# A hybrid decoder step: branch A's products behind the C tiles, gate A's as filler, the sample states' update in four row tiles

## The chip, the cores and the metric

The kernel runs on one core of one Trainium2 chip. The metric is the device time of one execution in microseconds. A profiled execution gives a span, from the first instruction to the last, and a time of its own, which is a little longer. TensorE (PE) multiplies, VectorE (DVE) and ScalarE (ACT) do the elementwise work, GpSimd (POOL) and SyncE (SP) issue most of the transfers.

## The reference

One layer of a decoder for 288 positions (256 of a new prompt, and 8 samples of 4 new tokens each), in float32. One projection of the normalised input gives the channels of both branches and their gates; all weights are read once, so the work is large products with 288 columns. Cut to what matters here:

```python
h = rmsnorm(x, norm1_g)
s_in, z, xbc, dt_raw, ga, gb = split(h @ w_in)
ya = sgu_branch(s_in, ...)                     # branch A: u * (W_s LN(v) + b)
yb, h_new, ... = mamba_branch(z, xbc, dt_raw, conv_buf, h0, ...)   # branch B: conv, SSD scan, gate, norm
merged = sigmoid(ga) * (ya @ w_out_a) + sigmoid(gb) * (yb @ w_out_b)
x = x + merged @ w_o
# SwiGLU feed-forward, final norm
```

For each of the 8 samples, 64 heads and a state of 64 x 128 per head, the recurrent state is also brought up to date over the sample's 4 tokens: the old state times the decay over the four tokens, plus the sum over the tokens of (decayed x dt) times B. This is some 16 MB read and as much written:

```python
h_fin = dec[..., None, None] * h + states     # states = einsum over the tokens of b, decay, x * dt
```

## The kernel before

**Float32 products.** Each operand is split into a high half (a float32r cast) and a low half (the rest), and a product is three matmuls: high x high, low x high, high x low. Weights are split as they arrive: SP loads a block `raw` (128 x 4 x 256), ACT casts it to `wh`, DVE subtracts to `wl`. A tile of 256 output channels takes 16 blocks of 128 input channels, two halves and three matmuls: 96 matmuls of 288 columns into the PSUM tile `pm`. The input is in such halves too: `hh`/`hl` for h, `yah`/`yal` for branch A, `ybh`/`ybl` for branch B, `mgh`/`mgl` for the merged branches, `xgh`/`xgl` and `fh`/`fl` for the feed-forward.

**Order.** `_order` lists the tiles: v (branch A), dt and b, u, c (C of the scan), ga (gate A), A (branch A's projection), then x and z tiles of the eight head groups of branch B between b tiles, B (first half of branch B's projection, which needs groups 0 to 3), further x and z tiles, gb, and B's second half. The output projection and the feed-forward follow. `units` runs through this list and issues the matmuls of the tiles, one after the other. After every block of a tile it calls `side`, which gives each waiting generator (an evacuation, a head group's scan, a state update) one step. The class `Plan` keeps a clock for each engine, adds a cost for each instruction that it issues, and holds a generator back until what it needs is ready by these clocks: so the order of each engine's instructions is fixed when the program is built. In it a load is ready 4000 ns after the transfer clock (`load`, lines 196 to 199), whichever queue issues it, and issuing takes the queue no time. Matmuls then wait for what really arrives.

**Branch A and its gate.** `g_gate_a` leaves tanh of half the gate in `sga`; `g_a` multiplies the product of a tile with it on DVE (line 170 is the helper's) and stores it to `scr_a`. `g_b2` reads that back much later and adds branch B.

**Group scans.** `g_ssd(g)` prepares head group g and also stores, for the four tokens of the samples, B as `scr_bs` (32 x 128) and the weighted x as `scr_xs` (128 x 128). `g_pre` applies the old states (`yoff`, four column tiles of 32). `g_gate(g)` gates and normalises group g (its matmul pair `rms`) and makes `ybh` and `ybl`, which B's products read.

**The states' update.** `g_upd(g)` runs after the mark "late", that is beside gb, B's second half, the output projection and the feed-forward. It loads `scr_xs` and `scr_bs` three times each with SP, splits them into `sk` (halves stacked in 96 partitions), and masks B by sample into `bk` (96 x 8 x 128). For each pair of heads it loads 512 KB of state, `su`, makes two matmuls of 512 columns (`up`), and eight DVE operations of 128 x 128 that multiply the state with its decay (`etot`, a scalar per partition) and add. POOL stores the result to `new_ssm_s`.

Of the kernel before, what the change touches and what calls it, by code (L numbers as in the profile page):

```python
# [407 lines left out]
def trunk(ctx, tc, io):  # L408
    ND = 6
    K = Plan(ctx, tc, io)  # L410
    nc = tc.nc
# [235 lines left out]
    etot = K.const([128, 32, NB], "etot")  # L647

    def g_dt(ps):
# [71 lines left out]
        for j in range(4):  # L721
            for i in range(2):
# [131 lines left out]
    def g_ssd(g):  # L854
# [36 lines left out]
        K.store(io["scr_bs"][g], bt[0:32, 2])  # L891
# [26 lines left out]
        K.store(io["scr_xs"][g], xw)  # L918
# [105 lines left out]
    def g_upd(g):  # L1024
        yield ["late", f"fin{g}", f"upd{g - 1}"]
        yield from K.res("q", 2)
        yield from K.res("t", 2)
        xf, b3 = K.tmp([96, 512], "xf"), K.tmp([96, 3, 128], "b3")
# [6 lines left out]
        K.copy(sk[:, 0], xf)
        K.copy(bh, b3[:, 0])
        yield sk
        K.sub(sk[64:96, 0], xf[64:96], sk[64:96, 0].bitcast(F32))
        K.vcopy(b3[:, 1], bh.bitcast(F32))
        K.sub(b3[32:64, 1], b3[32:64, 0], bh[32:64].bitcast(F32))  # L1040
        sk = sk[:, 0]
        bk = K.q_now([NB, 128], f"bk{g}", F32R)[0:96]
        K.mul(bk, b3[:, 1].unsqueeze(1).to_broadcast([96, NB, 128]),
              cst[0:96, C_BM:C_BM + NB].unsqueeze(2).to_broadcast([96, NB, 128]))
        K.rel("t", 2)
        yield None
        for j in range(4):
            st = yield from K.q([NB, 128], f"su{g}{j}")
            K.load(st, io["st_p"][4 * g + j])
            yield st  # L1050
            yield from K.res("x", 2)
            pu = [K.ps(f"up{i}") for i in range(2)]
            bf = bk.rearrange("p b n -> p (b n)")
            for i in range(2):
                K.mm(pu[i], sk[:, 128 * j:128 * j + 128], bf[:, 512 * i:512 * i + 512], True, True, f32=False)
            yield [st] + pu
            for b in range(NB):
                K.stt(st[:, b], st[:, b], etot[:, 4 * g + j, b:b + 1], pu[b // 4][:, 128 * (b % 4):128 * (b % 4) + 128],
                      ALU.mult, ALU.add)
                if b == 3:  # L1060
                    yield None
            K.rel("x", 2)
            yield st
            K.store(io["new_ssm_s"][4 * g + j], st)
            K.drop()
        K.drop(2)
        K.have.add(f"upd{g}")
# [305 lines left out]
def _constants():  # L1373
    import numpy as np

    c = np.zeros((128, C_W), np.float32)
    i = np.arange(128)
    c[:, C_ID:C_ID + 128] = np.eye(128)
    c[:, C_TRI:C_TRI + 128] = i[:, None] <= i[None, :]
    c[:, C_ONE:C_ONE + 128] = 1  # L1380
    c[:, C_ONE + 128:C_ONE + 256] = c[:, C_TRI:C_TRI + 128]
    c[:, C_NEG:C_NEG + 128] = np.where(i[:, None] <= i[None, :], 0, -1e30)
    c[:, C_SUF:C_SUF + 128] = i[:, None] > i[None, :]
    s = i[:32]
# [9 lines left out]
    h = i[:64]  # L1394
    c[:64, C_PAR:C_PAR + 128] = h[:, None] % 2 == i[None, :] // 64
    c[:64, C_JM:C_JM + 32] = h[:, None] // 2 == s[None, :]
    c[:96, C_BM:C_BM + 8] = (i[:96, None] % 32) // 4 == i[None, :8]
    return c


def _layout(f):
# [35 lines left out]
    for n, c in enumerate(cols):  # L1437
# [12 lines left out]
    dev["st_p"] = ca(f["state_ssm"][0].reshape(8, 32, 128, 128).transpose(1, 2, 0, 3))  # L1450
# [41 lines left out]
```

## Time and profile before

| what | value |
|---|---|
| median of 3 runs | 2320.87 us (2320.67 to 2321.26) |
| the profiled execution's own time | 2320.45 us |
| its span | 2318.7 us |
| TensorE busy | 2304.2 us, 99% |
| VectorE busy | 1431.4 us, 62% |
| ScalarE busy | 1001.0 us, 43% |
| GpSimd busy | 88.7 us, 4% |
| transfers | 455.96 MB, 197 GB/s over the span |
| mean granted TensorE clock | 0.998 |

A group's row reads: line, engine, operation, output <- inputs, shapes, count, then busy time, mean ns of one, and the idle time ahead with what ended it. Rows by time give the start, the duration, and in brackets the idle time before and what ended it. A matmul's record lasts longer than its share of TensorE, since matmuls are pipelined: what one costs is read from the distance of starts. The rows of stretches give the busy time of each engine, the granted clock (PEclk, 1.00 is full), the share of the transfer engines and GB/s. Of a tile, the spread min/median/max of durations is in ns.

### The profile page before, as it was taken

The numbers are of one execution on the slowest core, as the hardware profiler recorded it, in microseconds if no ns is written. First come the engines' busy times: TensorE is split into PE (matmuls) and PEld (weight loads), VectorE is DVE, ScalarE is ACT, GpSimd is POOL, SyncE is SP. The second block draws the span as 40 slices with busy tenths as digits, with TensorE's granted clock in tenths as the row PEclk, the third lists the DMA queues.
The fourth block names the chain that finished last, engine by engine and source line by source line (L and its number), as shares of the span: only waits on it lengthen the run. The fifth ranks groups of instructions, "written<-read, shape, count | busy, mean of one in ns | idle before, by whom it ended". The sixth has DMA issues, their size and how long they took to land.

```text
span 2318.7 us, 42525 instructions
## 1 busy us (share of the span) xinstructions
PE 2304.2 (99%) x17571; PEld 2271.5 (98%) x17571; DVE 1431.4 (62%) x2216; ACT 1001.0 (43%) x1425; POOL 88.7 (4%) x187
## 2 busy tenths in 40 slices
PE   9999999999999989999999999999999999999999
PEld 8999999999999989999999999999999999999999
DVE  7687553446887875477865767766664444545444
ACT  6453433335654645455433334433333333333333
POOL 0000000001110000010000000000000000000000
PEclk9999999999999999999999999999999999999999
DMA  8465686666667556565567877676775555555654
GB/s 290 132 210 149 199 285 190 180 185 193 188 188 229 152 168 190 174 189 150 176 216 246 284 239 250 216 222 218 227 227 167 167 170 165 168 165 164 229 168 140
DMA packets 151106, 455.96 MB, mean 197 GB/s; under 512 B 20848, under 2 KB 40560, under 8 KB 150912
## 3 DMA queue, kind: packets, MB, share of 16 engines
q1 hardware_dynamic: 140528, 424.06, 59.5%
q0 software_dynamic: 9376, 27.62, 3.3%
q8 instruction: 137, 2.24, 0.4%
q10 hardware_dynamic: 1008, 1.58, 0.2%
q14 instruction: 57, 0.47, 0.1%
HBM read 421.65 MB, written 31.54 MB: 195 GB/s over the span
## 4 chain that ended last, share of the span: by engine, by line
PE 99%; DVE 1%; DMA 0%; ACT 0%; issue 0%; SPq 0%; ACTq 0%; DVEq 0%
PE pm L187 94%; PE y L187 1%; PE up L187 1%; PE fin L187 1%; PE yoff L187 1%; PE mix L187 0%; PE xt L193 0%; PE cb L187 0%; DMA x<-x 0%; DVE wl L152 0%; PE va L193 0%; PE rms L187 0%; PE btok L193 0%; DVE xs L170 0%; DVE acc L170 0%
## 5 line engine op out<-in xcount | busy, mean ns | idle before, releaser
L152 DVE TENSOR_TENSOR wl<-raw,wh 128x1024 fp32r<-128x1024 f32 (+2 forms) x700 | 835.1, 1193 | 830.3 <-ACT wh L183 822.8
L183 ACT CAST wh<-raw 128x1024 fp32r<-128x1024 f32 (+2 forms) x704 | 717.6, 1020 | 1094.6 <-PE pm L187 796.3
L187 PE MATMUL pm<-hh,wh 128*128 128x288 f32 x2128 | 632.5, 297 | 0.0
L187 PE MATMUL pm<-hl,wh 128*128 128x288 f32 x2128 | 627.6, 295 | 0.0
L187 PE MATMUL pm<-hh,wl 128*128 128x288 f32 x2112 | 623.8, 295 | 0.0
L187 PE MATMUL pm<-xgl,wh 128*128 128x288 f32 x1408 | 415.8, 295 | 0.0
L187 PE MATMUL pm<-xgh,wl 128*128 128x288 f32 x1408 | 415.8, 295 | 0.0
L187 PE MATMUL pm<-xgh,wh 128*128 128x288 f32 x1408 | 414.5, 294 | 0.6 <-DVE ff L152 0.6
L187 PEld LDWEIGHTS pm<-hh,wh 128*128 128x128 f32 x2128 | 400.1, 188 | 9.5 <-issue 8.1
L187 PEld LDWEIGHTS pm<-hl,wh 128*128 128x128 f32 x2128 | 399.7, 188 | 0.2
L187 PEld LDWEIGHTS pm<-hh,wl 128*128 128x128 f32 x2112 | 396.7, 188 | 0.2 <-DVE wl L152 0.2
L187 PEld LDWEIGHTS pm<-xgh,wh 128*128 128x128 f32 x1408 | 264.2, 188 | 1.5 <-issue 0.8
L187 PEld LDWEIGHTS pm<-xgl,wh 128*128 128x128 f32 x1408 | 264.7, 188 | 0.7
L187 PEld LDWEIGHTS pm<-xgh,wl 128*128 128x128 f32 x1408 | 264.4, 188 | 0.0
L187 PE MATMUL pm<-fl,wh 128*128 128x288 f32 x704 | 207.9, 295 | 0.0
L187 PE MATMUL pm<-fh,wl 128*128 128x288 f32 x704 | 207.8, 295 | 0.0
L187 PE MATMUL pm<-fh,wh 128*128 128x288 f32 x704 | 207.2, 294 | 0.0
L187 PE MATMUL pm<-ybh,wh 128*128 128x288 f32 x512 | 153.2, 299 | 6.1 <-ACT ybh L183 6.1
L187 PE MATMUL pm<-ybl,wh 128*128 128x288 f32 x512 | 152.5, 298 | 0.8 <-DVE ybl L152 0.8
L187 PE MATMUL pm<-ybh,wl 128*128 128x288 f32 x512 | 152.4, 298 | 0.0
L187 PEld LDWEIGHTS pm<-fl,wh 128*128 128x128 f32 x704 | 132.3, 188 | 0.0
L187 PEld LDWEIGHTS pm<-fh,wl 128*128 128x128 f32 x704 | 132.2, 188 | 0.0
(254 smaller groups left out, 2809.8 us busy)
## 6 DMA issues: line engine op xcount, KB each, us to landing
raw<-w_in SPq DMA_DIRECT2D x284, 512.0 KB, 4.0
raw<-w_gu SPq DMA_DIRECT2D x176, 512.0 KB, 3.9
raw<-w_d SPq DMA_DIRECT2D x75, 512.0 KB, 3.6
raw<-w_b SPq DMA_DIRECT2D x64, 512.0 KB, 4.4
st<-st_n SPq DMA_DIRECT2D x32, 512.0 KB, 6.3
raw<-w_a SPq DMA_DIRECT2D x32, 512.0 KB, 3.9
su<-st_p SPq DMA_DIRECT2D x32, 512.0 KB, 5.7
new_ssm_s<-su POOLq DMA_DIRECT2D x32, 512.0 KB, 3.4
```

What stands on the lines that cost most here:

```text
L152: self.nc.vector.tensor_tensor(out, a, b, op=op)
L183: self.nc.scalar.copy(out, a)
L187: self.nc.tensor.matmul(out, lhsT, rhs, start=start, stop=stop)
```

## The change

Three things are changed. First the order: A follows the c tiles at once, and the ga tiles are spread between the x and z tiles ahead of B; some x, z and b tiles change places with them. Since A now comes before its gate, `g_a` copies the product on ACT and stores it, and `g_gate_a` loads it back, multiplies it with the gate, and stores it to a new buffer `scr_g`, which `load_b2` reads.

Second the operands of the states' update: `g_ssd` splits x and B into halves itself (`xb`) and stores both halves; `g_upd` loads them into `xk` and `bk`, at partitions 32r + 4i for sample r (of four at a time) and the product's part i, with 36 loads on POOL's queue. They need no mask, since each sample has its own rows.

Third the update: states are kept transposed (`st_n`, state index in the partitions, heads in the columns). For each half of the samples four matmuls of 12 rows and 512 columns, one per sample in its own row tile and PSUM bank, replace the masked ones; DVE multiplies 128 x 1024 of state with a broadcast decay and adds 128 x 512 at a time. `etot` holds the decay of every head in all partitions, 512 columns instead of 256. The arrays `C_PAR`, `C_JM`, `C_BM` and `st_p` go.

```diff
@@ _order
-    o = run("v", 0, 8) + [("dt", 0), ("b", 0)] + run("u", 0, 8) + run("c", 0, 4) + run("ga", 0, 8) + run("A", 0, 8)
-    o += xs(0, 2) + [("b", 1)] + xs(2, 3) + zs(0, 1) + xs(3, 4) + zs(1, 4) + [("b", 2)] + xs(4, 6) + run("B", 0, 8)
-    o += [("b", 3)] + xs(6, 8) + zs(4, 8) + [("late", 0)] + run("gb", 0, 8) + run("B", 8, 16)
+    o = run("v", 0, 8) + [("dt", 0), ("b", 0)] + run("u", 0, 8) + run("c", 0, 4) + run("A", 0, 8)
+    o += xs(0, 1) + run("ga", 0, 1) + xs(1, 2) + [("b", 1)] + zs(0, 1) + xs(2, 3) + run("ga", 1, 3) + zs(1, 2) + xs(3, 4)
+    o += run("ga", 3, 5) + zs(2, 4) + [("b", 2)] + run("ga", 5, 8) + xs(4, 5) + run("B", 0, 8)
+    o += xs(5, 6) + [("b", 3)] + zs(4, 5) + xs(6, 8) + zs(5, 8) + [("late", 0)] + run("gb", 0, 8) + run("B", 8, 16)
@@ g_dt
-        K.mm(pe[:, 0:256], cst[0:64, C_PAR:C_PAR + 128], em.rearrange("p j b -> p (j b)"), True, True)
+        K.mm(pe, K.one[0:64], em.rearrange("p b h -> p (b h)"), True, True)
@@ g_ssd
-        K.store(io["scr_bs"][g], bt[0:32, 2])
-        K.store(io["scr_xs"][g], xw)
+        xb = K.tmp([128, 4, 128], "xb", F32R)
+        K.hilo(xb[0:32, 2], xb[0:32, 3], bt[0:32, 2])
+        K.store(io["scr_bs"][g].rearrange("a t n -> t a n"), xb[0:32, 2:4])
+        yield xw
+        K.hilo(xb[:, 0], xb[:, 1], xw)
+        K.store(io["scr_xs"][g].rearrange("a p c -> p a c"), xb[:, 0:2])
@@ g_upd
-        for r in range(3):
-            K.load(xf[32 * r:32 * r + 32].rearrange("t (j c) -> t j c", j=4), io["scr_xs"][g].rearrange("(j t) c -> t j c", j=4))
-            K.load(b3[32 * r:32 * r + 32, 0], io["scr_bs"][g])
...
-            for i in range(2):
-                K.mm(pu[i], sk[:, 128 * j:128 * j + 128], bf[:, 512 * i:512 * i + 512], True, True, f32=False)
-            yield [st] + pu
-            for b in range(NB):
-                K.stt(st[:, b], st[:, b], etot[:, 4 * g + j, b:b + 1], pu[b // 4][:, 128 * (b % 4):128 * (b % 4) + 128],
-                      ALU.mult, ALU.add)
+        xk, bk = K.q_now([2, 512], f"xk{g}", F32R), K.tmp([128, 2, 128], "bk", F32R)
+        for r in range(4):
+            for i, (a, b) in enumerate(((0, 0), (0, 1), (1, 0))):
+                o = slice(32 * r + 4 * i, 32 * r + 4 * i + 4)
+                for h in range(2):
+                    K.load(xk[o, h].rearrange("l (j c) -> l j c", j=4),
+                           io["scr_xs"][g, a].rearrange("(j h r l) c -> h r l j c", j=4, h=2, r=4)[h, r], nc.gpsimd)
+                K.load(bk[o], io["scr_bs"][g, b].rearrange("(h r l) n -> r l h n", h=2, r=4)[r], nc.gpsimd)
+        yield [xk, bk]
+        for h in range(2):
+            yield from K.res("q", 2)
+            st = [K.q_now([2, 512], f"su{g}{h}{i}") for i in range(2)]
+            for i, t in enumerate(st):
+                K.load(t, io["st_n"][g, :, 2048 * h + 1024 * i:2048 * h + 1024 * i + 1024].rearrange("p (b c) -> p b c", b=2))
+            for i, t in enumerate(st):
+                yield t
+                v = t.rearrange("p b (h d) -> p b h d", h=8)
+                e = etot[:, 4 * h + 2 * i:4 * h + 2 * i + 2, 8 * g:8 * g + 8]
+                K.mul(v, v, e.unsqueeze(3).to_broadcast([128, 2, 8, 64]))
+            yield from K.res("x", 4)
+            pu = [K.ps(f"up{r}") for r in range(4)]
+            for r in range(4):
+                o = slice(32 * r, 32 * r + 12)
+                K.mm(pu[r], bk[o, h], xk[o, h], True, True, f32=False)
+            yield st + pu
+            for i, t in enumerate(st):
+                for k in range(2):
+                    K.add(t[:, k], pu[2 * i + k], t[:, k])
+                K.rel("x", 2)
+                K.store(io["new_ssm_s"][g, :, 2048 * h + 1024 * i:2048 * h + 1024 * i + 1024].rearrange("p (b c) -> p b c", b=2), t)
+                yield None
+            K.drop(2)
@@ g_a, g_gate_a
-        K.stt(t, sga[u // 2][:, 2 * (u % 2):2 * (u % 2) + 2], 1.0, ps[:, :, 0:T], ALU.add, ALU.mult)
+        K.copy(t, ps[:, :, 0:T])
...
+        K.load(a, io["scr_a"][u])
+        K.act(t, ps[:, :, 0:T], AF.Tanh, scale=0.5)
+        K.rel("m")
+        yield [t, a]
+        K.stt(a, t, 1.0, a, ALU.add, ALU.mult)
+        K.store(io["scr_g"][u], a)
```

Three places of the built order show what moved. The first is DVE where group 3 becomes B's input: `ybl` is the low half that B's first products wait for, `acc` and `xs` are the convolution of an x tile, `m` and `cbm` the scan of a group, `wl` a weight split (one of 128 x 1024 serves 24 matmuls). Before:

```order
L170 SCALAR_TENSOR_TENSOR acc<-cb,cwh,acc 128x312 x4
L152 TENSOR_TENSOR wl<-raw,wh 128x1024
L170 SCALAR_TENSOR_TENSOR acc<-cb,cwh,acc 128x312
L170 SCALAR_TENSOR_TENSOR xs_7204<-xs_7204,vec,rbg 128x288 x2
L152 TENSOR_TENSOR xw<-xts,wds 128x128
L152 TENSOR_TENSOR cbm<-csm,css 128x64
L166 TENSOR_SCALAR cbm<-cbm 128x64
L170 SCALAR_TENSOR_TENSOR xs_7204<-xs_7204,vec,rbg 128x288 x2
L152 TENSOR_TENSOR ybl_9419<-xs_7204,ybh_9418 128x576 x2
L170 SCALAR_TENSOR_TENSOR xs_9086<-cb,acc 128x2x256
```

and with the change:

```order
L152 TENSOR_TENSOR wl<-raw,wh 128x1024
L170 SCALAR_TENSOR_TENSOR xs_7059<-xs_7059,vec,rbg 128x288 x4
L152 TENSOR_TENSOR wl<-raw,wh 128x1024
L170 SCALAR_TENSOR_TENSOR ga<-tga,ga 128x576
L152 TENSOR_TENSOR ybl_8562<-xs_7059,ybh_8561 128x576 x2
L152 TENSOR_TENSOR wl<-raw,wh 128x1024 x4
L170 SCALAR_TENSOR_TENSOR ga<-tga,ga 128x576
L152 TENSOR_TENSOR wl<-raw,wh 128x1024 x4
L170 SCALAR_TENSOR_TENSOR ga<-tga,ga 128x576
```

`ybl` of group 3 stood among the convolution of the x tile directly ahead of B and the scan of the group after it; now gate tiles stand around it, and further weight splits of tiles that come before B follow it.

The second is POOL at the change from one group's update to the next, here from the first (stores of `su`) to the second. Before, POOL only stored:

```order
L202 DMA new_ssm_p<-fin 128x512
L202 DMA new_ssm_s<-su_12842 128x1024
L202 DMA new_ssm_s<-su_12988 128x1024
L202 DMA new_ssm_s<-su_13200 128x1024
L202 DMA new_ssm_s<-su_13370 128x1024
```

and with the change, where the last two rows come twelve times in all, before the next group's stores:

```order
L202 DMA new_ssm_s<-su_12872 128x1024
L202 DMA new_ssm_s<-su_12873 128x1024
L202 DMA new_ssm_s<-su_13112 128x1024
L202 DMA new_ssm_s<-su_13113 128x1024
L197 DMA xk_13310<-scr_xs 4x4x128 x2
L197 DMA bk<-scr_bs 4x2x128
```

The loads of a group's operands, which were on SP, now stand on POOL behind the four state stores of the group before.

The third is DVE in the update, from the second batch of one group (`su_13569`, `su_13570`) to the first of the next (`su_13842`, `su_13843`):

```order
L152 TENSOR_TENSOR su_13569<-su_13569,etot 128x1024
L152 TENSOR_TENSOR su_13570<-su_13570,etot 128x1024
L152 TENSOR_TENSOR wl<-raw,wh 128x1024
L152 TENSOR_TENSOR su_13569<-up_13667,su_13569 128x512
L152 TENSOR_TENSOR su_13569<-up_13668,su_13569 128x512
L152 TENSOR_TENSOR su_13570<-up_13669,su_13570 128x512
L152 TENSOR_TENSOR su_13570<-up_13670,su_13570 128x512
L152 TENSOR_TENSOR wl<-raw,wh 128x1024 x5
L152 TENSOR_TENSOR su_13842<-su_13842,etot 128x1024
L152 TENSOR_TENSOR wl<-raw,wh 128x1024
L152 TENSOR_TENSOR su_13843<-su_13843,etot 128x1024
L152 TENSOR_TENSOR wl<-raw,wh 128x1024
```

where before stood, for two pairs of heads of one group:

```order
L152 TENSOR_TENSOR wl<-raw,wh 128x1024 x3
L170 SCALAR_TENSOR_TENSOR su_13646<-su_13646,etot,up_13714 128x128 x4
L170 SCALAR_TENSOR_TENSOR su_13646<-su_13646,etot,up_13715 128x128 x4
L152 TENSOR_TENSOR wl<-raw,wh 128x1024 x5
L170 SCALAR_TENSOR_TENSOR su_13783<-su_13783,etot,up_13863 128x128 x4
L170 SCALAR_TENSOR_TENSOR su_13783<-su_13783,etot,up_13864 128x128 x4
```

The multiplication with the decay now stands ahead of the additions that need the matmuls, and seven weight splits stand between a group's last additions and the next group's first.

More of the change, by code (lines that the diff above doesn't have):

```diff
@@ L646, in trunk @@
     ecs = K.const([128, 64], "ecs")
-    etot = K.const([128, 32, NB], "etot")
+    etot = K.const([128, NB, 64], "etot")
     def g_dt(ps):
@@ L733, in g_dt @@
         K.rel("x", 2)
-        em = K.tmp([64, 32, NB], "em")
-        K.mul(em, et.unsqueeze(1).to_broadcast([64, 32, NB]),
-              cst[0:64, C_JM:C_JM + 32].unsqueeze(2).to_broadcast([64, 32, NB]))
+        em = K.tmp([64, NB, 64], "em")
+        K.mul(em, et.unsqueeze(2).to_broadcast([64, NB, 64]),
+              cst[0:64, C_ID:C_ID + 64].unsqueeze(1).to_broadcast([64, NB, 64]))
         yield em
@@ L739, in g_dt @@
         pe = K.ps("etot")
-        K.mm(pe[:, 0:256], cst[0:64, C_PAR:C_PAR + 128], em.rearrange("p j b -> p (j b)"), True, True)
+        K.mm(pe, K.one[0:64], em.rearrange("p b h -> p (b h)"), True, True)
         yield pe
-        K.copy(etot, pe[:, 0:256].rearrange("p (j b) -> p j b", j=32))
+        K.copy(etot, pe.rearrange("p (b h) -> p b h", b=NB))
         K.rel("x")
@@ L1035, in g_upd @@
[L1035 to L1053, printed above, removed]
-            for i in range(2):
-                K.mm(pu[i], sk[:, 128 * j:128 * j + 128], bf[:, 512 * i:512 * i + 512], True, True, f32=False)
-            yield [st] + pu
-            for b in range(NB):
-                K.stt(st[:, b], st[:, b], etot[:, 4 * g + j, b:b + 1], pu[b // 4][:, 128 * (b % 4):128 * (b % 4) + 128],
-                      ALU.mult, ALU.add)
[L1060 to L1065, printed above, removed]
@@ L1066, in g_upd @@
-        K.drop(2)
+        yield from K.res("q")
+        yield from K.res("t")
+        xk, bk = K.q_now([2, 512], f"xk{g}", F32R), K.tmp([128, 2, 128], "bk", F32R)
[6 more added lines that the diff above has]
+                K.load(bk[o], io["scr_bs"][g, b].rearrange("(h r l) n -> r l h n", h=2, r=4)[r], nc.gpsimd)
@@ L1067, in g_upd @@
+        K.drop()
+        K.rel("t")
         K.have.add(f"upd{g}")
@@ L1134, in g_a, with g_gate_a @@
         K.rel("t")
-        if u % 2:
-            K.drop()
         if u == 7:
             K.drop(8)
+        K.have.add(f"a{u}")
+    def g_gate_a(u, ps):
+        yield f"a{u}"
+        yield from K.res("t", 2)
+        t, a = K.tmp([128, 2, T], "tga"), K.tmp([128, 2, T], "ga")
+        K.load(a, io["scr_a"][u])
[4 more added lines that the diff above has]
+        K.store(io["scr_g"][u], a)
+        K.rel("t", 2)
     def g_b1(u, ps):
@@ L1164, in load_b2 @@
         ta, tb = K.tmp([128, 2, T], "la"), K.tmp([128, 2, T], "lb")
-        K.load(ta, io["scr_a"][u])
+        K.load(ta, io["scr_g"][u])
         K.load(tb, io["scr_b"][u])
@@ L1449, in _layout @@
     dev["st_n"] = ca(st.transpose(1, 3, 0, 2).reshape(8, 128, 4096))
-    dev["st_p"] = ca(f["state_ssm"][0].reshape(8, 32, 128, 128).transpose(1, 2, 0, 3))
     return dev
 _OUT = {
-    "y": (128, 16, T), "new_ssm_p": (8, 128, 512), "new_conv": (128, 48, 27), "new_ssm_s": (32, 128, 8, 128), "new_v": (32, 2048),
+    "y": (128, 16, T), "new_ssm_p": (8, 128, 512), "new_conv": (128, 48, 27), "new_ssm_s": (8, 128, 4096), "new_v": (32, 2048),
 }
-_SCR = {"scr_cs": (64, T), "scr_a": (8, 128, 2, T), "scr_b": (8, 128, 2, T),
-        "scr_xs": (8, 128, 128), "scr_bs": (8, 32, 128),
+_SCR = {"scr_cs": (64, T), "scr_a": (8, 128, 2, T), "scr_g": (8, 128, 2, T), "scr_b": (8, 128, 2, T),
+        "scr_xs": (8, 2, 128, 128), "scr_bs": (8, 2, 32, 128),
         "scr_xd": (8, 128, 2, 512), "scr_bt": (8, 128, 2, 128)}
@@ L1472 @@
     for n, s in _SCR.items():
-        io[n] = nc.dram_tensor(n, s, F32, kind="Internal").ap()
+        io[n] = nc.dram_tensor(n, s, F32R if n in ("scr_xs", "scr_bs") else F32, kind="Internal").ap()
     with tile.TileContext(nc) as tc, ExitStack() as ctx:
@@ L1479 @@
     sp = o["new_ssm_p"].reshape(8, 128, 4, 128).transpose(0, 2, 1, 3)
-    ss = o["new_ssm_s"].transpose(2, 0, 1, 3)
+    ss = o["new_ssm_s"].reshape(8, 128, NB, 512).transpose(2, 0, 3, 1)
     cv = o["new_conv"].transpose(2, 1, 0).reshape(27, 6144)
```

25 lines of the change are left out of this document (5 added, 20 removed).

## The prediction, made before the result was known

> **What bounds the kernel now.** I read the page first, then who TensorE waited for, then the stretch around its longest wait.
>
> ```profile
> span 2318.7 us, 42525 instructions
> PE 2304.2 (99%) x17571; PEld 2271.5 (98%) x17571; DVE 1431.4 (62%) x2216; ACT 1001.0 (43%) x1425; POOL 88.7 (4%) x187
> DMA  8465686666667556565567877676775555555654
> ...
> PE 99%; DVE 1%; DMA 0%; ACT 0%; issue 0%; SPq 0%; ACTq 0%; DVEq 0%
> ...
> PE pm L187 <- ACT ybh L183: 6.1, 1, 6.1
> PE pm L187 <- DVE ybl L152: 0.8, 1, 0.8
> PE pm L187 <- DVE ff L152: 0.6, 1, 0.6
> ```
>
> TensorE is the bound from end to end: the chain that ends last is TensorE for 99%, and no DMA or other engine holds it. So a change pays only by taking products off TensorE or by removing one of its few waits, and anything that makes TensorE wait is paid in full. The one large wait is for `ybh`, the high half of branch B's normalised input, at the first product of the first B tile.
>
> ```profile
> core 0: us, PE busy (x) PEld busy (x) DVE busy (x) ACT busy (x) POOL busy (x), PEclk, DMA share, GB/s
> 827.70:841.00 13.30, 13.30 (x104) 13.30 (x103) 10.91 (x22) 7.53 (x14) 2.37 (x6) 1.00 0.53 158
> 841.00:854.73 13.73, 6.81 (x28) 6.26 (x27) 10.56 (x24) 3.16 (x5) 1.26 (x3) 0.63 0.52 169
> ...
> 848.00:852.00 4.00, 3.21 (x14) 3.19 (x14) 3.66 (x10) 1.44 (x3) 0.00 (x0) 0.50 0.23 85
> ...
> 1350.83 20.72 PE pm L187 x156
> ```
>
> The last row gives the pitch of a 288-column product: 20.72 / 156 = 0.1328 us. From 841.00 to 854.73 only 28 products started; at the pitch they take 3.7 us, so this wait costs 13.73 - 3.7 = 10.0 us, of which 6.1 + 0.8 = 6.9 is idle and 3.1 is the granted clock of 0.50 that followed it. The profiled execution took 2320.45 us around its span of 2318.7; the median of the runs is 0.4 above it.
>
> **The change part by part. (1) The order.** In the built order of before, 54 of these products stand between the `rms` pair of group 3 (the last group that the first half of B needs) and B's first product, with group 4's SSD on DVE in between; now 450 stand there, 60 us instead of 7, and the gate tiles among them bring DVE one operation each where an x tile brings nine. The wait should go: -10.0. Branch A starts four C tiles behind the last u tile, 4 x 96 x 0.1328 = 51 us of cover for `ya`. I cost A's move, its ACT copy in place of a DVE operation, and eight more 288 KB stores and loads at nothing: DVE is at 62%, ACT at 43%, the DMA slices mostly at five to seven tenths. If that cover failed, the worst is that the 10.0 stays.
>
> **(2) Row tiles.** What an update product costs now, and what sharing the array does, is in TensorE's rows by time:
>
> ```profile
> 1161.52 0.62 PE L187 MATMUL up<-bk,sk 96*128 96x512 f32 x2
> 1161.97 0.30 PE L187 MATMUL pm<-hh,wh 128*128 128x288 f32 x1
> ...
> 288.29 0.30 PE L187 MATMUL pm<-hh,wl 128*128 128x288 f32 x1
> 288.51 1.93 PE L187 MATMUL yoff<-st,cm 128*32 128x512 f32 x16
> 290.37 0.40 PE L187 MATMUL pm<-hh,wh 128*128 128x288 f32 x1
> ...
> L187 PE MATMUL yoff<-st,cm 128*32 128x512 f32 x128 | 15.4, 598 | 0.0
> L187 PE MATMUL etot<-em,cst 64*128 64x256 f32 x2 | 0.7, 428 | 0.0
> ```
>
> Two `up` products hold TensorE from 1161.52 to 1161.97, 0.225 each (0.23 taken): 64 x 0.23 = 14.7 us. No row tile is in this trace; the nearest row is `yoff`, four column tiles of 32: 16 records of 598 ns in 1.86 us, so four run beside each other, with 0.22 in place of 0.13 before the first, 0.09 for entering. I take a batch of four row tiles as one product plus 0.09 on either side and 0.02 for three more starts: 0.43; 16 batches make 6.9: -7.8. The other end, tiles that run one after the other: 64 x 0.23 + 16 x 0.18 = 17.6: +2.9. `etot` doubles its columns: two records of 0.43 become 0.86 at most, +0.4 to +0.9; 0.4 taken.
>
> **(3) The operands by 36 loads on POOL's queue.** Before, the operands of a group came by six loads on SP's queue and were split and masked on ACT and DVE. Now they come as 36 loads of 4 or 8 KB on POOL, issued behind the group before's last state store, which waits for the last DVE addition of that group. The second batch of group g-1 and the first batch of group g stand 168, 156, 180, 192, 144, 192 and 192 products apart on TensorE (groups 1 to 7, counted in the built order): 22.3, 20.7, 23.9, 25.5, 19.1, 25.5 and 25.5 us at the pitch, 162.5 together. The code that places them books a load as landed 4 us on and gives POOL's issue no time. What the rows give:
>
> ```profile
> 658.68 1.10 POOL L202 DMA_DIRECT2D new_conv<-ncv  x2 [0.30 <-POOL ncv L763]
> 659.77 0.54 POOL L202 DMA_DIRECT2D scr_xd<-xd  x1
> 660.29 0.54 POOL L202 DMA_DIRECT2D scr_bt<-bt  x1
> ...
> L202 POOL DMA_DIRECT2D scr_bs<-bt x8: 511/511/513, 562.3 to 1044.0; - x8
> DMA to landing us min/median/max: 1.7/3.7/6.1
> ...
> 1162.71 2.15 DVE L170 SCALAR_TENSOR_TENSOR su<-su,etot,up 128x128 f32<-128x128 f32 x8
> 1165.16 0.54 POOL L202 DMA_DIRECT2D new_ssm_s<-su  x1 [102.39 <-DVE su L170]
> ...
> L152 DVE TENSOR_TENSOR wl<-raw,wh 128x1024 fp32r<-128x1024 f32 x663 | 811.2, 1224 | 795.7 <-ACT wh L183 788.3 <-DMA b<-scr_bs 4.0 <-PE pm L187 1.9
> L152 DVE TENSOR_TENSOR xt<-xt,dtk 128x512 f32<-128x512 f32 x16 | 10.9, 683 | 1.2 <-PE xt L193 1.2
> L152 DVE TENSOR_TENSOR bk<-b,cst 96x1024 fp32r<-96x1024 f32 x8 | 9.8, 1221 | 0.3
> ```
>
> POOL issues one DMA after another 0.52 to 0.55 us apart; the smallest, `scr_bs`, takes 0.511. So 36 loads take 36 x 0.51 = 18.4 us to issue. The 16 KB transfers of `scr_bs`, in both directions, land 1.7 to 6.1 us after issue, median 3.7. From the second batch to the last store lie on DVE the four additions (four of the `xt` row's 0.68: 2.7 us), and in most groups ahead of them two multiplications by `etot` (the `bk` row's 1.22 each) and one or two weight splits of 1.22: between 3.3 and 8.3 us; before, the same way took 1165.16 - 1161.52 = 3.6. I take 7, near the upper end, since in the built order the multiplications stand directly ahead of the additions. The need is then 7 + 0.5 (the store) + 18.4 + 3.7 = 29.6 us a group, against 22.3, 20.7, 23.9, 25.5, 19.1, 25.5 and 25.5: TensorE waits 7.3 + 8.9 + 5.7 + 4.1 + 10.5 + 4.1 + 4.1 = 44.7 us. Group 0 waits for nothing: its loads go out behind the last `new_ssm_p` store, over 400 products, 53 us, ahead. The waits don't make up for each other, since each group's loads start from its predecessor's own second batch.
>
> Each wait can lose the clock too: the one of 6.9 us did, for 3.1 us, and `ff`'s 0.6 did not. Three waits are longer than 6.9: 9.3; the other four I take at 0.8 each, between 0 and 3.1: together +12, between 0 and 22.
>
> By the Trainium skill ("TensorE: Matmul & The Clock Gate", Part 1), an idle stretch of about 3.4 us can already halve the clock until a busy one of that length; that speaks against this change, for it would put all seven waits at 3.1 us, 22 in place of 12, and the sum 10 us higher. The trace has one case, and it agrees.
>
> The Trainium skill ("DMA: Bandwidth & Descriptors", Anatomy of one DMA) fits a DMA of POOL's queue as 2.0 us and its bytes at 436 GB/s. That makes 2.0 in place of 3.7, and the sum 7 x 1.7 = 12 us lower, 2348; the row's median disagrees, its minimum of 1.7 doesn't.
>
> **(4) DVE and SP** do less: 256 operations of 0.34 us become 32 of 1.22 and 64 of 0.68 (87 to 83 us); SP loses 48 small loads and gains eight of 288 KB. Neither is on the path.
>
> The sum: 2320.45 - 10.0 - 7.8 + 0.4 + 44.7 + 12 = 2359.8, and 2360 for the median. Low end of the need: 5.5 on DVE and landing in 2.6 make 27.0, waits of 4.7, 6.3, 3.1, 1.5, 7.9, 1.5, 1.5 = 26.5, clock 3: 2333. High end: below, 2423.
>
> **The rivals. The ring of eight.** Each POOL load waits for the one eight before it, through eight semaphores. Up to a landing of 8 x 0.51 = 4.1 us this costs nothing; at 5.5 us the pitch becomes 0.69, the issue 24.8, the need 7 + 0.5 + 24.8 + 5.5 = 37.8, the waits 265 - 162.5 = 102, with 18 of clock: 2423. For it: `scr_bs` up to 6.1 and DMA slices at seven and eight tenths in this part; against it: the median. Chance 0.2.
>
> **The loads hide.** A load of 16 rows might be issued faster than any DMA in the trace. Then the first two parts are left: at 0.30 us apiece the need is 7 + 0.5 + 10.8 + 3.7 = 22.0, waits 0, 1.3, 0, 0, 2.9, 0, 0 = 4: 2320.45 - 17.4 + 4 = 2307. It decides from a need of 25 us, 0.38 us a load, where waits and clock eat the gain. Against it: 128 rows took 0.537 and 32 took 0.511, so rows are not what costs. Chance 0.1.
>
> **The tiles don't overlap** (+10.7 on the sum): 2371. For it: no row of row tiles; against it: `yoff`. Chance 0.1. **The wait at B only moves** (+10.0): 2370, if DVE's work of groups 3 and 4 falls behind elsewhere. Against it: DVE still had 18% idle in the stretch ahead of the wait. Chance 0.05.
>
> **How the numbers follow.** The forecast has 0.55, and says 2360 with its own range 2333 to 2390. The 0.8 range leaves out the hidden loads and the worst of the ring: 2331 to 2415. A change under 0.2% (4.6 us) cannot be told from none here. Slower by more has the forecast, the ring, the serial tiles and the moved wait, less the low tail of the forecast: 0.87. The hidden loads give faster, 0.08; the need near 25 us gives no change, 0.05.
>
> **What would show it.** Part 1: no wait for `ybh` near 840, clock 1.00 there, `gb` started 10 us earlier. Part 2: `up` records with 12 rows, four starting within 0.05 us. Part 3: TensorE's waits list DMA `xk` or `bk` seven times, 4 to 10 us each; POOL busy with 36 issues 0.51 us apart in each group; granted clock 0.50 for a few us behind the long waits; DVE, ACT and DMA no busier. I am wrong if TensorE has no such waits (the loads hidden), if POOL's issues stand further apart than 0.55 (the ring, or a dearer load), or if the loss shows ahead of 1120 us.

## The result, and the profile after

The changed kernel takes 2412.18 us (median of 4 runs, 2411.09 to 2414.12) against 2320.9: slower, ratio 1.0394, 95% interval 1.0377 to 1.0410, 91 us. The forecast was 2360, 39 us slower, range 2331 to 2415. The sign, the place and the cause are as forecast; the loss is more than twice as large. The profiled execution took 2411.09 us.

The page of the changed kernel:

```profile
span 2409.4 us, 42743 instructions
...
PE 2326.6 (97%) x17571; PEld 2280.7 (95%) x17571; DVE 1425.1 (59%) x2040; ACT 1004.0 (42%) x1433; POOL 258.8 (11%) x483
...
PEclk9999999999999999999988888899999999999999
...
PE 86%; DMA 6%; issue 5%; POOL 3%; DVE 0%; ACT 0%; SPq 0%; POOLq 0%; ACTq 0%
```

The chain that ends last was 99% TensorE; now 14% of it is DMA, POOL and issue. The granted clock is down in slices 21 to 26 alone, 1200 to 1570 us, where the sample states are updated. By stage (each row: stretch, length, the busy time of each engine, granted clock, DMA share, GB/s), before and then after:

```profile
840.00:870.00 30.00, 23.08 (x167) 21.91 (x165) 20.32 (x39) 11.64 (x23) 2.14 (x4) 0.83 0.52 167
...
1110.00:1560.00 450.00, 449.40 (x3356) 447.11 (x3353) 307.61 (x500) 184.12 (x221) 11.18 (x21) 1.00 0.72 230
```

```profile
840.00:870.00 30.00, 30.00 (x260) 28.75 (x259) 17.07 (x25) 16.41 (x34) 1.11 (x2) 1.00 0.58 179
...
1110.00:1560.00 450.00, 376.12 (x2648) 358.79 (x2647) 266.65 (x332) 142.45 (x175) 179.62 (x318) 0.89 0.66 214
```

The stall at 840 us is gone (TensorE busy 30.00 of 30). Between 1110 and 1560 TensorE has 2648 products where before it had 3356. Whom it waits for, by the list of waits:

```profile
PE up L187 <- DMA bk<-scr_bs: 45.9, 13, 5.9
PE up L187 <- DMA xk<-scr_xs: 20.9, 4, 7.1
PE up L187 <- issue: 6.0, 3, 2.5
...
PE pm L187 <- DVE xgl L152: 1.0, 1, 1.0
```

The three entries at `up` make 72.8 us, all in the first batches of groups 1 to 7. For 66.8 of them the list names `xk` or `bk`; for the other 6.0 it names nothing ("issue"). One batch, the first of group 5, on TensorE by time, with POOL's queue beside it:

```profile
1410.41 0.29 PE L187 MATMUL pm<-mgh,wl 128*128 128x288 f32 x1
1410.63 0.50 PE L187 MATMUL up<-xk,bk 12*128 12x512 f32 x1
1414.81 0.76 PE L187 MATMUL up<-xk,bk 12*128 12x512 f32 x1 [3.68 <-DMA bk<-scr_bs]
1421.48 0.76 PE L187 MATMUL up<-xk,bk 12*128 12x512 f32 x1 [5.91 <-DMA bk<-scr_bs]
1425.95 0.76 PE L187 MATMUL up<-xk,bk 12*128 12x512 f32 x1 [3.71 <-DMA bk<-scr_bs]
1426.64 0.61 PE L187 MATMUL pm<-mgh,wh 128*128 128x288 f32 x1
```

```profile
1394.93 0.53 POOL L202 DMA_DIRECT2D new_ssm_s<-su  x1 [12.40 <-DVE su L152]
1396.13 0.53 POOL L202 DMA_DIRECT2D new_ssm_s<-su  x1 [0.66 <-DVE su L152]
1396.65 1.18 POOL L197 DMA_DIRECT2D xk<-scr_xs  x2
...
1401.94 0.57 POOL L197 DMA_DIRECT2D xk<-scr_xs  x1 [1.29 <-DMA new_ssm_s<-su]
...
1408.57 1.14 POOL L197 DMA_DIRECT2D xk<-scr_xs  x2 [1.95 <-DMA xk<-scr_xs]
...
1423.64 0.56 POOL L197 DMA_DIRECT2D bk<-scr_bs  x1
```

Group 4's last state store is issued at 1396.13; the first of group 5's 36 loads follows at 1396.65 and the last at 1423.64, 27 us later; the last of the four row tiles starts at 1425.95. The first tile does not wait; the other three wait one after another, each for its own nine loads. Two of the load issues shown have an idle time in brackets: POOL itself waited. The first is the eighth load, and what it waited for is the store eight places ahead of it: in the trace POOL's 425 DMAs carry eight semaphores in turn. Read so for groups 1 to 7, with the parts that the prediction used (each from the start of one row to the start of the next; the wait is the time from the last product ahead of the batch to the first behind it, less a product of 0.13 and an unstalled batch of 0.52; the need runs from the second batch to the last tile, and the distance is what of it TensorE fills with products):

| group | second batch to last store | store | first to last load issue | last issue to last tile | need | distance | wait |
|---|---|---|---|---|---|---|---|
| 1 | 8.6 | 0.8 | 26.2 | 2.1 | 37.7 | 23.4 | 14.4 |
| 2 | 5.9 | 0.7 | 23.1 | 2.0 | 31.6 | 21.3 | 10.6 |
| 3 | 7.2 | 0.6 | 26.0 | 2.1 | 35.8 | 24.4 | 11.5 |
| 4 | 8.4 | 0.5 | 25.3 | 2.1 | 36.3 | 26.0 | 10.4 |
| 5 | 5.2 | 0.5 | 27.0 | 2.3 | 35.1 | 19.7 | 15.6 |
| 6 | 9.9 | 0.6 | 25.4 | 2.1 | 38.0 | 26.0 | 12.1 |
| 7 | 9.9 | 0.6 | 25.1 | 2.2 | 37.8 | 26.0 | 11.9 |
| sum | 55.1 | 4.3 | 178.0 | 14.8 | 252.2 | 166.9 | 86.5 |

Each of the seven waits also lost the clock. Around group 5:

```profile
1398.00:1408.00 10.00, 10.00 (x77) 10.00 (x76) 5.46 (x6) 4.28 (x5) 7.15 (x13) 1.00 0.98 307
...
1416.00:1426.00 10.00, 0.81 (x2) 0.36 (x2) 0.99 (x2) 0.00 (x0) 6.47 (x12) 0.50 0.51 163
1426.00:1434.00 8.00, 8.00 (x40) 7.56 (x41) 2.09 (x3) 1.05 (x1) 0.56 (x1) 0.65 0.24 96
```

From 1426 to 1434 TensorE runs again, but 40 products start where 60 would at 0.133. Over the seven groups the products started at half clock cost 1.7, 2.5, 2.3, 2.4, 2.2, 1.9 and 2.3 us more than 0.1328 each, 15.3 together.

The books: -10.0 (`ybh`), -6.3 (64 x 0.23 against 16 x 0.525), +0.4 (`etot`), +86.5 (waits), +15.3 (clock), and +2.8 for DVE three times a little late (0.6 and 1.2 us in the second batches of groups 0 and 7, 1.0 at `xgl`): 88.7 of the 90.6 between the two profiled executions; 1.9 is not located.

### The profile page after: what moved, and what is told of

Same layout as the page of the kernel before. It is cut to its first block, busy times and chain, and to the rows that moved or that the text cites. A ratio compares the mean times of both kernels' runs of the same rounds, so it can differ in the third digit from the quotient of the medians.

```text
span 2409.4 us, 42743 instructions
## 1 busy us (share of the span) xinstructions
PE 2326.6 (97%) x17571; PEld 2280.7 (95%) x17571; DVE 1425.1 (59%) x2040; ACT 1004.0 (42%) x1433; POOL 258.8 (11%) x483
## 4 chain that ended last, share of the span: by engine, by line
PE 86%; DMA 6%; issue 5%; POOL 3%; DVE 0%; ACT 0%; SPq 0%; POOLq 0%; ACTq 0%
PE pm L187 81%; DMA xk<-scr_xs 3%; POOL xk L197 2%; PE y L187 1%; DMA bk<-scr_bs 1%; DMA su<-st_n 1%; POOL bk L197 1%; DMA new_ssm_s<-su 1%; PE fin L187 1%; PE yoff L187 1%; PE mix L187 0%; PE xt L193 0%; POOL new_ssm_s L202 0%; PE cb L187 0%; DMA x<-x 0%
## 5 line engine op out<-in xcount | busy, mean ns | idle before, releaser
L187 PE MATMUL pm<-fh,wh 128*128 128x288 f32 x704 | 207.2, 294 | 0.0
```

The lines of the kernel that those rows point to most:

```text
L187: self.nc.tensor.matmul(out, lhsT, rhs, start=start, stop=stop)
```

## Experiments

The theory: TensorE waits because the 36 loads of a group are issued only behind its predecessor's last state store and take some 26 us to issue, part of it POOL's own time and part the eight semaphores of the queue. The rivals: the new order has a share; the tiles or DVE's work cost more than their rows show; POOL's issue time alone, without the eight, or the landing, or the bytes make the need.

**The order alone** on the kernel before, with `g_a`, `g_gate_a`, `load_b2` and `scr_g` as in the change:

```diff
-    o = ... + run("c", 0, 4) + run("ga", 0, 8) + run("A", 0, 8)
+    o = ... + run("c", 0, 4) + run("A", 0, 8)
+    o += xs(0, 1) + run("ga", 0, 1) + xs(1, 2) + ...
```

> The kernel before with part (1) alone: the new order, branch A's product stored and gated later by scr_g; the update of the sample states is the old one. Theory (the wait for ybh goes, all the rest of part 1 is covered): no wait for ybh near 840 us, granted clock 1.00 there, 2320.9 - 10.0 = 311 above 2000, that is 2311 us, between 2309 and 2313. Rival (the cover fails, the wait only moves): a wait of 5 us or more somewhere ahead of 1120 us, 2318 to 2322 us.

2311.07 us against 2320.69, ratio 0.9958 (0.9943 to 0.9973): -9.6 us where -10.0 was expected. In its list of waits the longest entry is 1.5 us, at the warm-up. Part 1 does what it says, and its cover held.

**The update alone**, the changed kernel with the order of before:

```diff
-    o += xs(0, 1) + run("ga", 0, 1) + xs(1, 2) + ...
+    o = ... + run("c", 0, 4) + run("ga", 0, 8) + run("A", 0, 8)
```

> The changed kernel with the order of before: parts (2) and (3) alone. Theory (the loss is all in the update, and the two parts do not touch each other): the wait for ybh is back, seven first batches wait 10 to 16 us each as in the changed kernel, and the time is 2412.2 + 10.0 = 2422 us, between 2418 and 2426. Rival (the new order has a share in the loss, for instance through later SSD work on DVE): 2412 us or less, with waits at the first batches that are shorter than in the changed kernel.

2431.61 us, ratio 1.0477 (1.0463 to 1.0492): 19.4 more than the changed kernel, not 10. So the order has no share in the loss, but the parts are not independent. TensorE's waits in it:

```profile
PE up L186 <- DMA bk<-scr_bs: 47.7, 13, 6.6
PE up L186 <- DMA xk<-scr_xs: 27.3, 5, 8.0
PE pm L186 <- ACT ybh L182: 8.3, 1, 8.3
...
PE rms L186 <- ACT rmp L182: 1.6, 1, 1.6
...
PE rms L186 <- DVE rmp L151: 1.5, 1, 1.5
PE pm L186 <- DVE ybl L151: 1.1, 1, 1.1
```

The old wait for `ybh` is longer than before, 8.3 in place of 6.1, with 3.1 us at the `rms` pair ahead of it: in `g_ssd` the new update splits `bt` and `xw` into `xb` on ACT and DVE, ahead of the work that `ybh` waits for. That this is the reason is argued from the code, not shown. By the same count as in the prediction (841 to 863 us, 53 products) this place now loses 15 us, not 10. And the first batches stand 161 us apart in all, not 162.5, with waits of 91.1. Together, 5 + 4.6, they come close to the 9.4 beyond what was expected.

**The placing code told a later landing**, so that the same loads get 30 us more of products in front of the batch:

```diff
+        for x in (xk, bk):
+            K.rdy[x.tensor.name] += 30000
         yield [xk, bk]
```

> The changed kernel, with 30 us more in the landing time that the placing code books for xk and bk; the same instructions, the first batch of each group stands some 30 us further behind its loads on TensorE. Theory (the loss is the wait for the operands and the clock lost behind it, and nothing else): no wait for xk or bk, no granted clock of 0.50 in this part, and 2320.9 - 10.0 (order) - 6.3 (16 batches of 0.52 in place of 64 x 0.23) + 0.4 (etot) = 2305 us, between 2303 and 2309. Rival (the 36 small loads also slow other transfers, or the tiles or DVE cost more than their records show): waits of TensorE elsewhere in this part, 2315 us or more.

2306.31 us, ratio 0.9937 (0.9925 to 0.9950). No wait for `xk` or `bk` is left, all sixteen batches cost 0.52 to 0.53, the clock stays at 1.00: the whole loss was the wait. It beats both kernels, by 14.4 and 106 us. Against the order alone it gains 4.8, where 6.3 - 0.4 was expected. The loads themselves still took 21.3 to 26.2 us from the first to the last issue, so nothing was made cheaper: it was covered.

**SP's queue for the 36 loads** (the scratch tensors as F32, the operands loaded under that type):

```diff
-                    K.load(xk[o, h]..., io["scr_xs"]...[h, r], nc.gpsimd)
+                    K.load(xk[o, h].bitcast(F32)..., io["scr_xs"]...[h, r])
-                K.load(bk[o], io["scr_bs"]...[r], nc.gpsimd)
+                K.load(bk[o].bitcast(F32), io["scr_bs"]...[r])
```

> The changed kernel with its 36 loads a group on SP's queue instead of POOL's, nothing else moved. [...] Theory (the ring binds too: eight loads in flight, each 4 to 5 us, so 36 take about 36 x 4.5 / 8 = 20 us on any queue): the 36 loads still take 16 to 24 us from first to last issue, the waits for xk and bk stay at 6 us or more, and weight loads queue behind them on SP, so TensorE waits for weights as well: 2400 to 2480 us. Rival (POOL's issue time alone makes the need): the 36 are issued within 6 us, the need falls by 20 us a group, the waits go, 2305 to 2312 us.

2345.84 us, ratio 1.0110 (1.0096 to 1.0124): neither. The rows of its `xk` issues, of its waits, and of two stretches (while group 4's 36 loads are issued, and behind them):

```profile
L197 SPq DMA_DIRECT2D xk<-scr_xs x192: 241/298/761, 1131.3 to 1469.2; - x192
```

```profile
PE pm L187 <- ACT wh L183: 7.4, 4, 2.9
PE pm L187 <- DVE wl L152: 6.3, 8, 1.8
...
PE up L187 <- DMA bk<-scr_bs: 1.7, 1, 1.7
```

```profile
1313.00:1327.00 14.00, 14.00 (x108) 14.00 (x107) 9.54 (x12) 3.83 (x4) 1.07 (x2) 1.00 0.39 137
1327.00:1337.00 10.00, 6.85 (x42) 6.35 (x40) 3.70 (x4) 2.28 (x3) 0.00 (x0) 0.89 0.85 297
```

An issue takes SP 0.298 us in the median. The rival's 6 us would need 0.17, and no row had shown that: the cheapest SP issue in the profile before took 0.31. The 36 took 13.1 to 16.9 us from first to last, in seven of the eight groups below the 16 to 24 of the theory and in all above the 6 of the rival. The operands are in time in all groups but one (1.7 us). The cost is elsewhere: meanwhile SP brings few weights (DMA share 0.39), and in the ten microseconds behind it TensorE is busy for 6.85, with waits for the split weights, while the share is 0.85. The theory's second half held (weights queue behind), its first didn't. SP's rows also say what the 36 spend their time on: two of them start 0.343 us apart in the median, 12.0 us for 35 steps, and the few steps longer than 0.40 hold the other 1.1 to 5.0. So on SP most of it is the issue itself.

**Smaller doses of the third experiment**, 8 and 10 us in place of 30, to see the waits and the clock at short waits:

```diff
+            K.rdy[x.tensor.name] += 8000     (10000 in the second)
```

> The changed kernel with 8 us more (not 30) in the landing time booked for xk and bk: in the built order the second batch and the next first one then stand 240, 222, 240, 204, 258, 264 and 228 products apart, 31.9, 29.5, 31.9, 27.1, 34.3, 35.1 and 30.3 us. Theory (need of 35 us, as the changed kernel shows it): waits of 3.1, 5.5, 3.1, 7.9, 0.7, 0 and 4.7, 25 us in all, 2305 + 25 = 2330 before the clock. On the clock the two views differ: if only a wait of more than 6.9 us loses it (the forecast's rule), one drop, 2 us, 2332; if some 3 us of idle are enough, five drops, 11 us, 2341.

> The same with 10 us more: 264, 234, 240, 222, 258, 264 and 252 products, 35.1, 31.1, 31.9, 29.5, 34.3, 35.1 and 33.5 us. Theory: with a need between 32 and 36 us the waits are 4 to 25 us in all, none above 6.5; at 34 they are 10 us. 2305 + 10 = 2315, between 2309 and 2335. If only a wait above 6.9 us loses the clock, none is lost here; if some 3 us are enough, two drops or so, 4 us more.

2364.11 us (ratio 1.0185, 1.0170 to 1.0200) and 2336.76 (1.0065, 1.0046 to 1.0084): both above what was expected. The waits were 2.4, 4.0, 11.6, 9.3, 3.7, 8.5, 5.9 (45.4 together) and 0.3, 3.6, 8.1, 6.1, 2.4, 4.0, 0.2 (24.6), where 25 and 10 were expected. The need had grown to a mean of 38.4 and 37.0 us: with shorter waits the last loads land later, 4.9 and 4.5 us from the last issue to the last tile in place of 2.1. In the changed kernel TensorE stands during that time and the DMA share falls (0.98 to 0.51 above); here the weight loads go on. That this is why they land sooner there is likely, but only argued.

The clock: seven drops that cost 11.6 us, and four that cost 8.8. So the forecast's rule (only above 6.9 us) is wrong, the other right: every wait of 3.6 us or more lost it (one of 2.9 too, in the last run of the next experiment), the two of 2.4 once each way, those of 0.3 and less never. The wait of 2.4 that did, on TensorE by time, and the stretch behind it:

```profile
1208.85 0.51 PE L187 MATMUL up<-xk,bk 12*128 12x512 f32 x3
1211.30 0.46 PE L187 MATMUL up<-xk,bk 12*128 12x512 f32 x1 [1.95 <-DMA xk<-scr_xs]
...
1212.06 0.43 PE L187 MATMUL pm<-hh,wl 128*128 128x288 f32 x1
```

```profile
1212.05:1215.47 3.42, 3.42 (x17) 3.42 (x16) 0.00 (x0) 1.03 (x1) 0.00 (x0) 0.50 0.93 316
1215.47:1218.00 2.53, 2.53 (x21) 2.53 (x21) 2.48 (x4) 0.02 (x1) 0.00 (x0) 1.00 0.43 162
```

Half clock begins 0.75 us behind the end of the wait and lasts 3.42 us. Behind the waits for `up` in all these runs the drops last 3.41, 6.83, 10.24, 13.65 or 17.07 us, whole multiples of 3.41. The Trainium skill ("TensorE: Matmul & The Clock Gate", Part 1) says that the gate looks at free-running windows of 3413 ns; these lengths agree. It also asks for one idle window of about 3.4 us before the clock falls; here 1.95 us of idle, between tiles that use 12 of the 128 rows, was enough once, so on that the measurement differs. The last full product ahead of this wait and the first behind it start 3.07 us apart (1208.62 and 1211.69); whether the clock counts the small tiles as work is not shown.

**24 loads in place of 36.** First by one load for both halves of `xk` (16 KB in place of two of 8):

```diff
-                for h in range(2):
-                    K.load(xk[o, h]..., io["scr_xs"][g, a]...[h, r], nc.gpsimd)
+                K.load(xk[o]..., io["scr_xs"][g, a].rearrange("(j h r l) c -> r l j h c", ...)[r], nc.gpsimd)
...
-                K.mm(pu[r], bk[o, h], xk[o, h], True, True, f32=False)
+                K.mm(pu[r], bk[o, h], xk[o, h::2], True, True, f32=False)
```

> The changed kernel with the two halves of xk taken by one load of 16 KB in place of two of 8 KB: 24 loads a group on POOL's queue in place of 36, the same bytes, the same places on TensorE (distances 22.3, 20.7, 23.9, 25.5, 19.1, 25.5 and 25.5 us). Theory (the need goes by the number of loads): 24 x 0.57 = 13.7, the ring 2 to 4, so need 7.9 + 0.6 + 16.5 + 2 = 27 us, waits 4.7 + 6.3 + 3.1 + 1.5 + 7.9 + 1.5 + 1.5 = 26.5, clock 5 to 15: 2305 + 26.5 + 10 = 2341 us, between 2330 and 2355. Rival (the bytes set the need: the larger loads take longer to issue or to land, and the ring gives the gain back): waits within 3 us of the changed kernel's, 2390 to 2412 us.

and then with `bk`'s 12 loads on SP and `xk`'s 24 of 8 KB on POOL:

> The changed kernel with the 12 loads of bk on SP's queue and the 24 of xk left on POOL's, in pieces of 8 KB; the same places on TensorE. Theory (number of loads on a queue, not bytes of one): POOL issues 24 loads in 14 to 18 us, the need falls to about 27 us as in the kernel with 24 loads of mixed size, and 12 loads are too few to hold the weight loads on SP up for long: 2335 to 2360 us. Rival (each SP load holds the weights up as the 36 did): TensorE waits for wh or wl for 5 us or more, 2360 to 2375 us.

2381.58 us (ratio 1.0263, 1.0247 to 1.0278) and 2369.70 (1.0203, 1.0186 to 1.0220). Waits of 55.7 and 45.0, clock 13.8 and 14.4. The need fell from 36.0 to 31.6 and 30.2 us, not to 27. From the first to the last issue they took 19.1 and 17.2 us where 23 x 0.57 = 13.1 is POOL's own time: the rest, 6.0 and 4.1, is nearly all waiting. POOL's issues and waits in the changed kernel, and then in the merged one:

```profile
L197 POOL DMA_DIRECT2D xk<-scr_xs x192: 566/576/668, 1114.2 to 1539.0; - x192
...
DMA to landing us min/median/max: 1.9/4.5/8.4
```

```profile
POOL bk L197 <- DMA xk<-scr_xs: 11.7, 17, 1.4
POOL xk L197 <- DMA xk<-scr_xs: 10.9, 17, 2.0
POOL xk L197 <- issue: 9.2, 10, 3.8
...
POOL xk L197 <- DMA new_ssm_s<-su: 4.9, 6, 1.3
POOL xk L197 <- DMA bk<-scr_bs: 2.9, 3, 1.6
```

```profile
L197 POOL DMA_DIRECT2D xk<-scr_xs x96: 585/595/650, 1113.7 to 1506.8; - x96
...
DMA to landing us min/median/max: 2.4/5.7/9.8
```

```profile
POOL xk L197 <- DMA xk<-scr_xs: 32.7, 33, 2.0
```

A load of twice the bytes costs POOL 0.02 us more, but lands later, a median of 5.7 in place of 4.5, and the waits of POOL's loads for earlier loads and stores rise from 30.4 us to about 38 although there are a third fewer. So the eight semaphores bind, and they bind by the landing. (The "issue" entry is another matter; the part on the prediction comes to it.) Twelve issues less are 6.8 us; the need fell by 4.4 and 5.8. Neither the theory's 2341 nor the rival's 2390 came: the number of loads sets the larger part, the landing takes some of it back. The 12 loads on SP held no weights up: no wait for `wh` or `wl` of 0.5 us is in TensorE's list of waits there.

**The loads a group ahead:**

```diff
+    def g_opl(g):
+        yield ["late", f"fin{g}", f"half{g - 1}"]
+        ...the 36 loads, into a second pair of xk, bk...
     def g_upd(g):
-        yield ["late", f"fin{g}", f"upd{g - 1}"]
+        yield ["late", f"opl{g}", f"upd{g - 1}"]
...
         yield [xk, bk]
+        K.have.add(f"half{g}")
```

> The changed kernel with the 36 loads of group g+1 put on POOL's queue as soon as group g's own operands are there, ahead of group g's state stores and into a second pair of buffers, in place of behind them. The same loads, and the groups now stand closer together on TensorE than in the changed kernel: 132, 114, 114, 144, 120, 126 and 132 products between the second batch and the next first one, 117 us together in place of 162. Theory (TensorE waited because the loads were issued behind the predecessor's last store; a whole group's time, some 35 us, covers the 26 us of issue and the landing): waits of 0 to 2 us in all, no granted clock of 0.50, 2306 us, between 2304 and 2312. Rival (POOL's queue is full, so the stores behind the loads hold the state buffers back and TensorE waits for DVE or for su instead): waits of 3 us or more a group, 2325 us or more.

2308.44 us, ratio 0.9948 (0.9936 to 0.9961). Its waits at `up`:

```profile
PE up L187 <- DMA bk<-scr_bs: 0.8, 1, 0.8
```

From the first to the last issue these loads took 22 to 32 us, longer than in the changed kernel, and the groups stand closer, 117 us in place of 162. The loads are the same and no faster, only their start has moved ahead of the store, and the wait is gone: what cost 102 us (86.5 of waits, 15.3 of clock) is where they stood, behind the store.

**Only the leading part**, 12 loads (the two correcting products of the update left out):

```diff
-            for i, (a, b) in enumerate(((0, 0), (0, 1), (1, 0))):
+            for i, (a, b) in enumerate(((0, 0),)):
...
-                o = slice(32 * r, 32 * r + 12)
+                o = slice(32 * r, 32 * r + 4)
```

> The changed kernel with only the leading part of the three (high half times high half): 12 loads a group in place of 36, four rows a tile in place of twelve; the two correcting products of the update are left out. The same places on TensorE. Theory (the need goes by the number of loads, 0.57 us each, and by the ring, which can bind only behind the eighth): 7.9 + 0.6 + 6.3 + a ring of 1 to 3 + a landing of 3 to 6 = 19 to 24 us against 22.3, 20.7, 23.9, 25.5, 19.1, 25.5 and 25.5: waits only in groups 1, 2 and 5, 0 to 9 us together, 2305 to 2318 us. Rival (the start of the loads behind the state store, or their landing, is what costs, whatever their number): five waits or more, 2330 us or more.

2312.84 us, ratio 0.9965 (0.9951 to 0.9978). From first to last issue 6.2 to 9.0 us, waits of 0.2 and 1.8 in groups 1 and 5, no clock lost. With the places on TensorE unchanged, a third of the loads takes the loss away: the store ahead of them and the landing alone do not make it. The 6.5 us to the third experiment are these 2.0, the 2.8 that DVE is late also in the changed kernel (there the batches were moved away from those places), and 1.7 not located.

## Why the prediction was right in kind and too small

**Part 1** was right: no wait for `ybh`, 9.6 us gained alone against 10.0. What it costed at nothing (A's move, the extra stores and loads) cost nothing that shows. One reading was off without touching the sum: the wait for `ybh` is not at the first product of the first B tile, which starts at 831.4 us, but 72 products later, at 847.4, where the tile first reads group 3's half. It saw no tie to part 2; there is one, 5 us, that only shows with the old order.

**Part 2**: the tiles do run beside each other. An unstalled batch's four products start within 0.01 us of each other, and the batch costs 0.52, not 0.43: 0.09 us on entering, as taken, and 0.42 from the tiles' start to the next product, where one product of 0.23 with 0.09 and 0.02 had been taken. The gain is 6.3, not 7.8. `etot` is +0.4, as taken. The rival of serial tiles is out.

**Part 3** had the place and the chain right and failed in its largest term, the issue: 36 x 0.51 = 18.4 us, with the reason "Up to a landing of 8 x 0.51 = 4.1 us this costs nothing" and 3.7 us as the landing. The runs show 26.0 in its place. The forecast had the eight semaphores, gave them as a rival (need 37.8, waits 102, 2423) and set them aside because a median lay below a bound. Two things are wrong in that. The landing was 4.5 in the median, and a median is no bound: landings ran from 1.9 to 8.4, POOL issues in order, so each late one holds up all behind it, and early ones give nothing back. By terms, over seven groups, against 29.6 each:

- 36 issues: POOL took at least 0.566 us for an `xk` load of 4 rows, not the 0.511 of a 32-row store. The forecast had taken the cheapest row of the trace as what a load costs; +2.0 a group, 14 us.
- POOL standing between the issues: 26.0 us from the first issue to the end of the last, less 36 x 0.566 = 20.4: +5.6 a group, 39 us. This is the largest term of what was missing, and it shows where the forecast had said that it would be wrong, in issues that stand further apart than 0.55. By POOL's rows 28.9 of the 39 us ended with the landing of the load or store eight places ahead. Another 9.3 ended with nothing that the profile shows, 7.6 of them in two pauses, in groups 3 and 6, that no part of the forecast had:

```profile
1298.29 1.14 POOL L197 DMA_DIRECT2D xk<-scr_xs  x2 [3.82 <-issue]
```

  The DMA eight places ahead of this load had landed 3.2 us before it started. So the semaphores account for some 29 of the 39 us; what the pauses are stays open.
- the landing of the last load: the last tile starts 1.5 us behind the end of the last issue, where 3.7 had been taken: -15 us.
- DVE and the store: 8.5 us, not 7.5: +7 us.

14 + 39 - 15 + 7 = 45: the need is 252.2 us in place of 207.2, and as the distances were right (162.5 counted, 166.9 by time, with the products at half clock in them) nearly all of it became waiting, 86.5 in place of 44.7. That the waits don't make up for each other also held. That the rival's 2423 came close is in part luck: its issue of 24.8 us was too short, its 5.5 for the last landing too long. And group 0 waited for nothing, but with less to spare than forecast: its loads started 35 us ahead of its first batch, not 53.

The clock was forecast at 12 and cost 15.3. The forecast's rule, 3.1 us for a wait over 6.9 and little for the others, was wrong in both halves: a drop cost 1.4 to 2.6 us in the changed kernel and the two doses, and waits from 2.9 us on all had one. The alternative, that all seven lose 3.1, was right on how often and too high on how much.

**Part 4**, "neither is on the path", was nearly right: 2.8 us of waits for DVE.

The rival "the loads hide" supposed a cheaper issue; it was dearer. "The wait at B only moves" is out by the first experiment.

## What to carry to other kernels

Many small DMAs on one queue cost their number times the queue's issue time, and beyond that every late landing, as soon as the outstanding ones are limited: take the spread of the landings, not the median, and compare it with the limit times the pitch. If such loads must be small, start them a stage ahead: the same 36 loads, issued no faster, cost 102 us or nothing here, by where they stood relative to one store. A placing code that books a transfer's landing but not its issue will put the consumer too early: booking 30 us more for these loads, in two lines, turned a loss of 91 us into a gain of 14, while 8 and 10 us more were not enough.

## What the runs showed of the hardware that was not expected

- POOL needed 0.56 to 0.58 us to issue a load of 4 rows and 4 or 8 KB, more than the 0.53 for a 512 KB state store; 16 KB cost 0.595.
- POOL paused, with no releaser in the profile, at its 120th, 241st and 362nd DMA: 2.4, 3.8 and 3.8 us in the changed kernel. In the third experiment and in the one with the loads a group ahead the pauses stand at the same three DMAs (2.4 to 2.8 us), in the merged kernel at the 116th and 237th (2.5 and 2.9): each time 121 apart. In the third experiment the DMA eight places ahead had landed 3.4 to 4.8 us before. What they are is not shown.
- Whether loads of 8 KB land later because the DMA engines are busy stays open. In the third experiment the 36 loads of groups 3, 4 and 5 (rows: stretch, busy times, clock, DMA share, GB/s) were issued in 26.2, 21.6 and 21.6 us; summing what each issue stood further than 0.60 us behind the one before, POOL waited 6.2, 1.8 and 1.8 of it, but 2.5 of the 6.2 are a pause as above:

```profile
1350.00:1377.00 27.00, 27.00 (x206) 27.00 (x205) 15.61 (x20) 10.70 (x12) 20.56 (x37) 1.00 0.79 231
1427.00:1449.00 22.00, 22.00 (x168) 22.00 (x167) 14.75 (x22) 9.47 (x12) 20.06 (x36) 1.00 0.72 217
1500.00:1523.00 23.00, 23.00 (x175) 23.00 (x175) 12.60 (x16) 8.36 (x10) 20.76 (x37) 1.00 0.73 221
```

  In the changed kernel the share was 0.98 at the head of group 5's loads, where the same sum is 6.9. But at the head of group 6's it was nearly as high, and there landings cost POOL 1.5 us:

```profile
1453.00:1469.00 16.00, 16.00 (x123) 16.00 (x122) 9.28 (x12) 6.44 (x8) 10.43 (x19) 1.00 0.93 318
```

  No run changed the share alone. The Trainium skill ("DMA: Bandwidth & Descriptors", Anatomy of one DMA) gives a DMA of this queue about 2.0 us and its bytes at 436 GB/s; the smallest landings, 1.8 and 1.9, agree, the medians of 4.2 and 4.5 do not.
- A wait of 2.4 us, 1.95 of it idle, was enough to halve the clock once, and once not; the half clock always lasted a multiple of 3.41 us.
